# Attention products of two heads at a time with feature-major results, and a limit on how many weight units are asked for ahead of a loop

## The chip, the cores and the metric

The kernel runs on one core of a Trainium2 chip. The core has five engines with queues of their own: TensorE (PE, with its weight loads shown apart as PEld), VectorE (DVE), ScalarE (ACT), GpSimd (POOL) and SyncE (SP), and 16 DMA engines. The metric is device time in microseconds (us): the median of several runs, lower is better.

## The reference

Two blocks on 256 tokens of 1024 features, in float32. The first is a diffusion-style block: a gated feed-forward network, a mixer and another feed-forward network. Its mixer adds a gated recurrence (split here into products within and between chunks) and a windowed attention with 8 query heads on 2 key heads, whose keys are the 128-token band and 256 context tokens:

```
s_band = einsum('bkgnqd,bknsd->bkgnqs', qb, kb) * scale        # where(valid), and s_ctx on the context
p = softmax_with_sink(concatenate([s_band, s_ctx]), sink)
o = einsum(p[..., :3*BLOCK], vb) + einsum(p[..., 3*BLOCK:], vc)
```

The second block runs two layers. Each has four attention branches side by side (latent attention of 4 heads, stick-breaking attention of 4, sliding-window attention with sinks of 8 heads on 2 key heads, differential attention of 4), gates and merges them, normalizes, and sends each token to 2 of 32 experts:

```
merged = gate_a * (o_a @ w_br_a) + gate_b * (o_b @ w_br_b) + gate_c * (o_c @ w_br_c) + gate_d * (o_d @ w_br_d)
x = layer_norm(DN_ALPHA * x + merged @ w_out);  x = layer_norm(DN_ALPHA * x + grouped_moe(x))
```

## The kernel before

Tokens lie as two tiles of 128 (index `i`). Weights come from memory in units of 128 x 1024 floats (512 KB). The class `Weights` keeps a list of all units in the order of use. `_load` asks for the next unit as soon as a slot (a buffer) is free, on SP's DMA queue; `_prepare` splits a unit into a high part (ACT, L97) and a low part (DVE or POOL, L98) where products are made of three passes (`mm3`, L151 to L153); `more` gives slots back. The units of the experts are used unsplit.

A scheduler sets the order of instructions on each engine before the run. It places projections (L151 to L153), which wait for nothing but weights, between the steps of the attention.

*First block.* `attention(i)` goes head by head: scores of one head (L835; K is 64 rows, so half the rows of the array, upper for s = 0, lower for s = 1), mask, maximum, exponential (L838 to L844), four transposes (L847), a copy, four products with the values (L851: 128 stationary columns, 64 moving ones), all heads into one PSUM tile with tokens on partitions. At the end one multiplication divides by the softmax sums, and `rows_T` transposes the result to feature-major for the output projection. `within(i)`, the recurrence inside chunks (L877 to L913), is a second generator that is drawn three steps for each head. Both take PSUM tiles of the tag `ax`, of which there are four.

*Second block.* In each layer the sliding window (L1258, L1272), the differential part (L1296, L1315), the stick-breaking part (L1339, L1340, L1360) and the latent part (L1413, L1420) write token-major results into `OT[i]`; after the gates they are transposed (L1453) and split.

*Experts.* `expert_pass` handles 8 quads of 4 experts, 24 units a quad: `prepare` gathers tokens by a one-hot product (L1624, L1633), `first` (L1662) and `second` (L1689) put four experts side by side, each on 32 columns of the array. There are 41 slots for units. After the fourth quad (unit 96) `more_rounds` reads a count into a register on all engines and runs a loop for experts with more than 32 tokens; in these runs the loop's body is not entered, but SP must have its loads landed and all engines meet there (L1753, L1754). SP's part of that stands behind the loads that were asked for by then:

```
with tc.issue_after(st.loads[st.taken + 8].ins):
    nr = nc.values_load(rounds[0:1, 0:1], min_val=0, max_val=S // CAP - 1)
with tc.For_i(0, nr, 1):
```

Of the kernel before, what the change touches and what calls it, by code (L numbers as in the profile page):

```python
# [18 lines left out]
D = 1024  # L19
# [5 lines left out]
ETB = 2  # L25
QUADS = 8
RING3 = 12
# [4 lines left out]
class Weights:  # L32
# [4 lines left out]
    def __init__(self, nc):  # L37
        self.nc = nc
        self.seq = []
        self.free = {"raw": deque(), "split": deque()}  # L40
        self.loaded = self.ready = self.taken = 0
        self.raw, self.parts, self.held, self.out = {}, {}, {}, []
        self.names = 0
        self.loads = []
        self.end = {}
# [76 lines left out]
def build(tc, A, out):  # L122
# [203 lines left out]
    def gate_rows(pool, i, r, w):  # L326
# [6 lines left out]
        return G  # L333

# [492 lines left out]
    def attention(i):  # L827
        nm = pa.tile([128, 8], FT, name="nmax", bufs=2)
        den = pa.tile([128, 8], FT, name="den", bufs=2)
        PO = pmm("ax")  # L830
        for j in range(4):
            for s in range(2):
                h = j + 4 * s
                P = pmm("ax")
                PE.matmul(P, lhsT=aqT[64 * s:64 * s + 64, j, 128 * i:128 * i + 128], rhs=akT[64 * s:64 * s + 64, :],  # L835
                          start=True, stop=True)
                mk = P[:, 128:256] if i == 0 else P[:, 0:128]
# [10 lines left out]
                pT = pa.tile([128, 512], FT, name="pT", bufs=2)  # L848
# [11 lines left out]
        V.tensor_tensor(out=o.rearrange("p (h d) -> p h d", h=8), in0=PO.rearrange("p (h d) -> p h d", h=8),  # L860
                        in1=den[:, :, None].to_broadcast([128, 8, 64]), op=OP.mult)
        rows_T(oaT, i, o)
# [274 lines left out]
    for l in range(2):  # L1137
# [10 lines left out]
        OT = [pL.tile([128, 1280], FT, name=f"o{i}") for i in range(2)]  # L1148
# [93 lines left out]
        project("swk", 1)  # L1242
        if l:
            rows_on()
        for i in range(2):
# [3 lines left out]

            PO = pmm("ax")  # L1250
            den = pa.tile([128, 8], FT, name="den", bufs=3)
            for s in range(2):
                for g0 in range(0, 4, per):
                    P = pmm("ax")
                    Pv = P.rearrange("p (a b) -> p a b", a=per)
                    sc = pa.tile([128, 512], FT, name="sc", bufs=2).rearrange("p (a b) -> p a b", a=per)
                    for j in range(per):
                        PE.matmul(Pv[:, j, :], lhsT=qs["swq"][64 * s:64 * s + 64, g0 + j, qsl],  # L1258
                                  rhs=qs["swk"][64 * s:64 * s + 64, 0, :keys], start=True, stop=True)
                    for j in range(per):  # L1260
                        V.scalar_tensor_tensor(sc[:, j, :], dist[:, 1, 128 * i:128 * i + keys], -sw_slopes[4 * s + g0 + j],
                                               Pv[:, j, :], op0=OP.mult, op1=OP.add)
# [6 lines left out]
                    T = transposed([pr[:, j, 128 * b:128 * b + 128] for j in range(per) for b in blocks(i)])  # L1269
                    for j in range(per):  # L1270
                        for b in blocks(i):
                            PE.matmul(PO[:, 64 * (h0 + j):64 * (h0 + j) + 64], lhsT=T[j * (i + 1) + b],  # L1272
                                      rhs=swv[:, b, 64 * s:64 * s + 64], start=b == 0, stop=b == i)
            V.reciprocal(den, den)
            V.tensor_tensor(out=OT[i][:, 512:1024].rearrange("p (h d) -> p h d", h=8), in0=PO.rearrange("p (h d) -> p h d", h=8),
                            in1=den[:, :, None].to_broadcast([128, 8, 64]), op=OP.mult)
# [7 lines left out]
        for i in range(2):  # L1284
            keys = 128 * (i + 1)
            qsl = slice(128 * i, 128 * i + 128)

            PO = pmm("ax")
            for g0 in range(4):
                n = 2  # L1290
                o = 32 * g0
                P = pmm("ax")
                Pv = P[:, :2 * keys].rearrange("p (a b) -> p a b", a=n)
                sc = pa.tile([128, 512], FT, name="sc", bufs=2)[:, :2 * keys].rearrange("p (a b) -> p a b", a=n)
                for j in range(n):
                    PE.matmul(Pv[:, j, :], lhsT=qs["dfq"][o:o + 32, j, qsl], rhs=qs["dfk"][o:o + 32, j, :keys],  # L1296
                              start=True, stop=True, tile_position=(o, 0))
# [19 lines left out]
            od = OT[i][:, 1024:1280]  # L1317
# [16 lines left out]
        aTs = []  # L1334
        for h in range(4):
            o = 64 * (h % 2)
            q_, k_ = qs["sbq"][o:o + 64, h // 2, :], qs["sbk"][o:o + 64, h // 2, :]
            P = pmm("ax")
            PE.matmul(P[:, 0:256], lhsT=k_[:, 0:128], rhs=q_, start=True, stop=True)  # L1339
            PE.matmul(P[:, 256:384], lhsT=k_[:, 128:256], rhs=q_[:, 128:256], start=True, stop=True)  # L1340
# [15 lines left out]
        for i in range(2):  # L1356
            PO = pmm("ax")
            for h in range(4):
                for b in blocks(i):
                    PE.matmul(PO[:, 64 * h:64 * h + 64], lhsT=aTs[h][:, 128 * (i + b):128 * (i + b) + 128],  # L1360
                              rhs=vv[:, b, 64 * h:64 * h + 64], start=b == 0, stop=b == i)
            V.tensor_copy(OT[i][:, 256:512], PO[:, :256])

# [38 lines left out]
        for i in range(2):  # L1402
# [6 lines left out]
            for g0 in range(0, 4, per):  # L1409
# [8 lines left out]
                for j in range(per):  # L1418
                    for b in blocks(i):
                        PE.matmul(PO[:, 64 * (g0 + j):64 * (g0 + j) + 64], lhsT=T[j * (i + 1) + b],  # L1420
                                  rhs=mv[:, b, 64 * (g0 + j):64 * (g0 + j) + 64], start=b == 0, stop=b == i)
            V.reciprocal(den[:, :4], den[:, :4])
            V.tensor_tensor(out=OT[i][:, 0:256].rearrange("p (h d) -> p h d", h=4), in0=PO[:, :256].rearrange("p (h d) -> p h d", h=4),
                            in1=den[:, 0:4, None].to_broadcast([128, 4, 64]), op=OP.mult)
# [23 lines left out]
        for k in range(0, 10, 2):  # L1448
            P = pmm("ax")
            for kk in range(2):  # L1450
                for i in range(2):
# [164 lines left out]
        def expert_pass(place, w13_of, w2_of, after, main):  # L1616
# [92 lines left out]
            for p in range(QUADS):  # L1709
# [40 lines left out]
        def more_rounds():  # L1750

            with tc.issue_after(st.loads[st.taken + 8].ins):
# [13 lines left out]

        expert_pass(place, taken, taken, st.more, True)
# [85 lines left out]
def layout(I):  # L1853
# [26 lines left out]
    for n, z in (("w_oa", I["w_o_attn"][0]), ("w_oh", I["w_o_hgrn"][0])):  # L1880
# [63 lines left out]
    for l in range(2):  # L1944
# [17 lines left out]
        b = np.concatenate([J["w_br_" + n][l] for n in "abcd"], 0)  # L1962
# [26 lines left out]
```

## Time and profile before

| | |
|---|---|
| median of 3 runs | 2072.26 us (2071.64 to 2073.36) |
| the profiled execution, its own time | 2079.71 us |
| its span, first to last instruction | 2077.9 us |
| mean granted TensorE clock | 0.947 of 2.4 GHz |
| busy: PE, DVE, ACT, POOL | 88%, 53%, 38%, 11% |
| read from memory | 433.51 MB, 209 GB/s over the span |

The profile lists instructions with line numbers of the kernel (L835 is line 835). An f32 matmul is two instructions there, so "x8" of them is four products. A matmul's duration includes its way through the array; consecutive ones overlap, so the cost of one is read from start to start. PEclk is the granted share of full clock, 1.00 for 2.4 GHz and 0.50 for 1.2 GHz.

### The profile page before, as it was taken

Reading aid. Unit: us, or ns where it says so; the run is one execution under the profiler, and the core shown is the slowest. Engines: PE = TensorE matmul, PEld = TensorE weight load, DVE = VectorE, ACT = ScalarE, POOL = GpSimd, SP = SyncE. Lnnn points to the kernel's source line nnn. Section 1 sums busy time; section 2 is a strip of 40 time slices with the busy share of each in tenths; the row PEclk is TensorE's granted clock in tenths of the full one; section 3 lists DMA queues with packets and bytes.
Section 4 is the critical chain, followed back from the end, with each engine's and each line's share of the span. In section 5 each row is a group of like instructions: output and inputs, shape, how many; then the busy total and the mean of one; then the engine's idle time right before and its main releaser. Section 6 shows DMA issues by size and latency. Waiting matters only on the chain. (4 is left out here: it accounts for less than half of the span.)

```text
span 2077.9 us, 29422 instructions
## 1 busy us (share of the span) xinstructions
PE 1823.1 (88%) x11398; PEld 1437.9 (69%) x11398; DVE 1098.2 (53%) x2088; ACT 788.1 (38%) x1363; POOL 238.1 (11%) x170
## 2 busy tenths in 40 slices
PE   6989999989999987999999997963979999988096
PEld 2767788877878786998888996522438899853052
DVE  4775465584656567554668556210257864631023
ACT  3443222453443435444445644210234574321011
POOL 2553000131132221000100011000010000200000
PEclk9999999999999999999999999986999999989598
DMA  8543565442232234555434378897964435889987
GB/s 310 193 149 119 187 234 205 147 157 82 71 125 82 72 103 143 185 190 189 146 113 135 122 265 321 345 413 302 414 241 142 132 123 203 305 333 413 377 338 280
DMA packets 120118, 436.61 MB, mean 210 GB/s; under 512 B 13616, under 2 KB 13664, under 8 KB 119968
## 3 DMA queue, kind: packets, MB, share of 16 engines
q1 hardware_dynamic: 116208, 422.63, 55.3%
q0 software_dynamic: 2608, 8.32, 1.2%
q10 hardware_dynamic: 1152, 3.67, 0.5%
q8 instruction: 94, 1.54, 0.3%
q14 instruction: 56, 0.46, 0.1%
HBM read 433.51 MB, written 1.05 MB: 209 GB/s over the span
## 5 line engine op out<-in xcount | busy, mean ns | idle before, releaser
L98 DVE TENSOR_TENSOR split7l<-raw,split7h 128x1024 fp32r<-128x1024 f32 x98 | 124.6, 1271 | 113.1 <-ACT split7h L97 112.9
L98 DVE TENSOR_TENSOR split6l<-raw,split6h 128x1024 fp32r<-128x1024 f32 x99 | 128.4, 1297 | 85.4 <-ACT split6h L97 82.4
L97 ACT ACTIVATE split6h<-raw 128x1024 fp32r<-128x1024 f32 x102 | 107.9, 1057 | 162.5 <-issue 58.9
L97 ACT ACTIVATE split7h<-raw 128x1024 fp32r<-128x1024 f32 x101 | 106.8, 1057 | 165.0 <-PE mm L153 65.4
L1633 PE MATMUL ax<-OH,X 128*128 128x128 f32 x512 | 71.7, 307 | 100.0 <-DVE OH L1624 97.9
L1633 PEld LDWEIGHTS ax<-OH,X 128*128 128x128 f32 x512 | 70.1, 222 | 105.1 <-DVE OH L1624 98.7
L1662 PE MATMUL ax<-raw,xg 128*32 128x512 f32 x1024 | 133.9, 595 | 4.1 <-DMA raw<-in_moe 4.1
L1662 PEld LDWEIGHTS ax<-raw,xg 128*32 128x32 f32 x1024 | 33.9, 109 | 91.3 <-issue 61.4
L586 DVE SCALAR_TENSOR_TENSOR xn<-raw,xn 128x1024 f32<-128x1024 f32 x56 | 84.9, 1517 | 22.0 <-DMA raw<-in_w_mod 21.3
L363 ACT ACTIVATE xg<-ax,cols 128x128 f32<-128x128 f32 x64 | 24.0, 456 | 176.6 <-PE ax L1633 176.6
L1689 PE MATMUL ax<-raw,ehT 128*32 128x512 f32 x512 | 70.7, 608 | 18.6 <-ACT ehT L144 17.7
L583 POOL TENSOR_TENSOR raw<-raw,xn 128x1024 f32<-128x1024 f32 x24 | 72.5, 3033 | 73.8 <-DVE xn L586 70.1
L1696 DVE SCALAR_TENSOR_TENSOR yl<-ax,gsl,yh 128x512 fp32r<-128x512 f32 x32 | 24.0, 751 | 87.4 <-ACT yh L1695 83.7
L1671 DVE TENSOR_TENSOR ehs<-ax,ehs 128x256 f32<-128x256 f32 x16 | 6.8, 424 | 117.5 <-ACT ehs L1670 117.5
L1624 DVE TENSOR_TENSOR OH<-iota,place 128x128 f32<-128x128 f32 x32 | 7.8, 286 | 110.8 <-SPq L1754 98.7
L1689 PEld LDWEIGHTS ax<-raw,ehT 128*32 128x32 f32 x512 | 16.7, 110 | 57.8 <-issue 28.0
L153 PE MATMUL mm<-hThi,split7l 128*128 128x512 f32 x128 | 52.5, 410 | 3.9 <-DVE split7l L98 3.9
L153 PE MATMUL mm<-hxhi,split7l 128*128 128x256 f32 x192 | 54.8, 286 | 1.3 <-POOL split7l L98 1.2
L151 PE MATMUL mm<-hxhi,split6h 128*128 128x256 f32 x192 | 54.5, 284 | 1.7 <-ACT split6h L97 1.7
L151 PE MATMUL mm<-hThi,split6h 128*128 128x512 f32 x128 | 51.7, 404 | 4.3 <-ACT hThi L144 2.2
L1670 ACT ACTIVATE ehs<-ax 128x256 f32<-128x256 f32 x16 | 6.1, 384 | 129.5 <-PE ax L1662 129.5
L152 PE MATMUL mm<-hxlo,split7h 128*128 128x256 f32 x192 | 54.7, 285 | 0.7 <-POOL hxlo L380 0.7
(876 smaller groups left out, 5776.3 us busy)
## 6 DMA issues: line engine op xcount, KB each, us to landing
raw<-in_moe SPq DMA_DIRECT2D x384, 512.0 KB, 10.1
raw<-in_f_in SPq DMA_DIRECT2D x88, 512.0 KB, 4.2
raw<-in_w_gate SPq DMA_DIRECT2D x64, 512.0 KB, 3.4
raw<-in_w_mod SPq DMA_DIRECT2D x56, 512.0 KB, 4.3
raw<-in_f_out SPq DMA_DIRECT2D x55, 512.0 KB, 4.2
raw<-in_w_out SPq DMA_DIRECT2D x24, 512.0 KB, 6.0
raw<-in_w_br SPq DMA_DIRECT2D x20, 512.0 KB, 3.5
raw<-in_w_ada SPq DMA_DIRECT2D x16, 512.0 KB, 10.0
```

The source lines that it names most:

```text
L97: nc.scalar.activation(hi, x, AF.Copy)
L98: (nc.gpsimd if self.seq[i][1] == "pool" else nc.vector).tensor_tensor(out=lo, in0=x, in1=hi, op=OP.subtract)
L151: PE.matmul(o, lhsT=lh, rhs=rh, start=first, stop=False)
L152: PE.matmul(o, lhsT=lh, rhs=rl, start=False, stop=False)
L153: PE.matmul(o, lhsT=ll, rhs=rh, start=False, stop=last)
L363: SC.activation(o, p, AF.Identity, bias=b, scale=g)
L583: GP.tensor_tensor(out=w, in0=w, in1=crow[r], op=OP.mult)
L586: V.scalar_tensor_tensor(mscr, w, 1.0, crow[r], op0=OP.mult, op1=OP.mult, accum_out=m)
L1633: PE.matmul(P[:, 128 * b:128 * b + 128], lhsT=X[:, i, 128 * d:128 * d + 128], rhs=OH[:, i, :], start=i == 0, stop=i == 1)
L1662: PE.matmul(P[32 * s:32 * s + 32, :], lhsT=xg[:, k, 32 * s:32 * s + 32], rhs=ws[s](kk), start=k == 0, stop=k == DT - 1, tile_position=(0, ...
L1689: PE.matmul(P[32 * s:32 * s + 32, :], lhsT=d_["hT"][:, k, 32 * s:32 * s + 32], rhs=ws[s](k), start=k == 0, stop=k == 1, tile_position=(0, ...
L1696: V.scalar_tensor_tensor(yl, P, d_["gsl"], yh, op0=OP.mult, op1=OP.subtract)
```

## The change

Five edits:

- The scores of two heads are issued one after the other before the softmax of either, in the first block (s = 0 and s = 1), the sliding window, the differential part (32-row tiles) and the stick-breaking part.
- The products with the values swap sides: the values (64 columns) are stationary, the transposed probabilities (128 columns) move, and the two heads of a pair write the upper and lower 64 partitions of one PSUM tile, features on partitions. In the latent part too.
- Division by the softmax sums moves behind that: `over_rows` spreads 1/sum over the partitions with small products (64 columns each), a copy on ACT and a multiplication on DVE. The transposes of these results go: `rows_T` in the first block, four of five groups at L1453. The results have tiles of their own (`swo`, `smo`); the output weights are laid out to match on the host.
- The generators of the first block are drawn 5 times with 6 steps of `within`, instead of 9 times with 3.
- `_load` stops at `limit`, which is set to 16 units beyond the fourth quad before the pass and lifted after the loop; SP's part of the loop stands behind the last of these.

```diff
+AHEAD = 16
     def _load(self):
-        while self.loaded < len(self.seq):
+        while self.loaded < min(len(self.seq), self.limit):
...
+    def over_rows(o, p, c, n):
+        R = pmm("ax")
+        for j in range(n):
+            for s in range(2):
+                PE.matmul(R[64 * s:64 * s + 64, 128 * j:128 * j + 128], lhsT=c[:, s, j:j + 1].to_broadcast([128, 64]), rhs=ident,
+                          start=True, stop=True, tile_position=(0, 64 * s))
+        copy_act(o, R[:, :128 * n].rearrange("p (a b) -> p a b", a=n))
+        V.tensor_tensor(out=o, in0=p.rearrange("p (a b) -> p a b", a=n), in1=o, op=OP.mult)
...
         for j in range(4):
-            for s in range(2):
-                h = j + 4 * s
-                P = pmm("ax")
+            Ps = [pmm("ax") for _ in range(2)]
+            for s, P in enumerate(Ps):
                 PE.matmul(P, lhsT=aqT[64 * s:64 * s + 64, j, 128 * i:128 * i + 128], rhs=akT[64 * s:64 * s + 64, :],
                           start=True, stop=True)
+            pTs = []
+            for s, P in enumerate(Ps):
+                h = j + 4 * s
...
-                for b in range(4):
-                    PE.matmul(PO[:, h * 64:h * 64 + 64], lhsT=pT[:, b * 128:b * 128 + 128], rhs=av[:, b, s * 64:s * 64 + 64],
-                              start=b == 0, stop=b == 3)
-                yield
+                pTs.append(pT)
+            for b in range(4):
+                for s in range(2):
+                    PE.matmul(PO[64 * s:64 * s + 64, 128 * j:128 * j + 128], lhsT=av[:, b, s * 64:s * 64 + 64],
+                              rhs=pTs[s][:, b * 128:b * 128 + 128], start=b == 0, stop=b == 3, tile_position=(0, 64 * s))
+            yield
...
-        rows_T(oaT, i, o)
+        over_rows(o, PO, den.rearrange("p (s j) -> p s j", s=2), 4)
...
-        for n in range(9):
+        for n in range(5):
             next(a)
-            for _ in range(3):
+            for _ in range(6):
                 next(w, None)
...
-        for k in range(0, 10, 2):
-            P = pmm("ax")
-            for kk in range(2):
-                for i in range(2):
-                    c = (k + kk) * 128
-                    PE.transpose(P[:, kk * 256 + i * 128:kk * 256 + i * 128 + 128], OT[i][:, c:c + 128], ident)
-            split(oT[k // 2][:, 0], oT[k // 2][:, 1], P.rearrange("p (a b) -> p a b", a=2))
+        P = pmm("ax")
+        for kk in range(2):
+            for i in range(2):
+                PE.transpose(P[:, kk * 256 + i * 128:kk * 256 + i * 128 + 128], OT[i][:, 128 * kk:128 * kk + 128], ident)
+        for t, o in zip(oT, (smo[:, 0:2], smo[:, 2:4], swo[:, 0:2], swo[:, 2:4], P.rearrange("p (a b) -> p a b", a=2))):
+            split(t[:, 0], t[:, 1], o)
...
                     more_rounds()
+                    st.limit = 1 << 30
+                    st.more()
                     prepare(p + 1)
...
-            with tc.issue_after(st.loads[st.taken + 8].ins):
+            with tc.issue_after(st.loads[st.limit - 1].ins):
...
+        st.limit = st.taken + 12 * QUADS + AHEAD
         expert_pass(place, taken, taken, st.more, True)
```

The sliding-window, differential, stick-breaking and latent parts change in the same way as `attention`.

Three places show what the scheduler makes of it. The first is SP's queue at the loop of the first layer. The numbers after `raw` are those of the slot and of the tile. Before, the last loads ahead of the loop are:

```order
L80 DMA raw34_12131<-in_moe 128x1024
L80 DMA raw0_12141<-in_moe 128x1024
...
L80 DMA raw26_12193<-in_moe 128x1024
L80 DMA raw37_12195<-in_moe 128x1024
L80 DMA raw38_12197<-in_moe 128x1024
L1753 TENSOR_LOAD rounds_11540
L1754 COMPARE_AND_BRANCH
```

After the change:

```order
L83 DMA raw32_12076<-in_moe 128x1024
L83 DMA raw46_12091<-in_moe 128x1024
L83 DMA raw47_12093<-in_moe 128x1024
L83 DMA raw48_12095<-in_moe 128x1024
L1790 TENSOR_LOAD rounds_11562
L1791 COMPARE_AND_BRANCH
```

25 loads that stood ahead of the loop stand behind it (the first of them into slot 49); 16 beyond unit 96 stay ahead. The second layer's loop is the same.

The second place is PE's order in a pair of heads of the first block's second half. `pr` are the probabilities, `pT` their transposes, `Mh`, `lfh` and `lfl` belong to `within`. Before, one head after its transposes, and the scores of the next:

```order
L847 MATMUL ax<-ident,pr 128x128 x4
L877 MATMUL ax<-Mh,lfh_3679 128x512
L878 MATMUL ax<-Mh,lfl_3680 128x512
L877 MATMUL ax<-Mh,lfh_3679 128x512
L878 MATMUL ax<-Mh,lfl_3680 128x512
L851 MATMUL ax<-av,pT 128x64 x4
L877 MATMUL ax<-Mh,lfh_3679 128x512
L878 MATMUL ax<-Mh,lfl_3680 128x512
L835 MATMUL ax<-akT,aqT 128x512
```

After, both heads' transposes (L865) and their eight products with the values (L871):

```order
L865 MATMUL ax<-ident,pr 128x128 x4
L155 MATMUL mm<-hxlo,split6h 128x256
L156 MATMUL mm<-hxhi,split6l 128x256
L865 MATMUL ax<-ident,pr 128x128 x4
L898 MATMUL ax<-Mh,lfh_3924 128x512
L871 MATMUL ax<-pT,av 64x128
L899 MATMUL ax<-Mh,lfl_3925 128x512
L898 MATMUL ax<-Mh,lfh_3924 128x512
L871 MATMUL ax<-pT,av 64x128 x7
L899 MATMUL ax<-Mh,lfl_3925 128x512
```

Two projections stand between the two heads' transposes; the value products of both heads form one group, cut once by a product of `within`.

The third place is PE's order at the end of the first block's attention (second half). Before, from the last but one head's values on:

```order
L851 MATMUL ax<-av,pT 128x64 x4
L901 MATMUL ax<-W,U 128x128 x4
L835 MATMUL ax<-akT,aqT 128x512
L847 MATMUL ax<-ident,pr 128x128 x4
L901 MATMUL ax<-W,U 128x128 x4
L851 MATMUL ax<-av,pT 128x64 x4
L901 MATMUL ax<-W,U 128x128 x4
L901 MATMUL ax<-qT,ksum 128x128 x4
L823 MATMUL ax<-ident,oatt 128x128 x4
L911 MATMUL ax<-hv_3506,AT 128x128
```

After, the products of `over_rows` (L344), the end of `within`, and projections behind it:

```order
L922 MATMUL ax<-qT,ksum 128x128 x4
L344 MATMUL ax<-ident,den 64x128 x8
L154 MATMUL mm<-hxhi,split7h 128x256
...
L932 MATMUL ax<-hv_3506,AT 128x128
L934 MATMUL ax<-S_3749,VS_4997 128x128
L934 MATMUL ax<-S_3974,VS_4999 128x128
L155 MATMUL mm<-hxlo,split7h 128x256
L156 MATMUL mm<-hxhi,split7l 128x256
L154 MATMUL mm<-hxhi,split7h 128x256
L155 MATMUL mm<-hxlo,split7h 128x256
```

Before, no projection is left there; after, 184 stand behind the attention's last product.

## Rows read from the trace of the kernel before

**Rows 1.** The page's first part: busy time, share, instructions.
```profile
PE 1823.1 (88%) x11398; PEld 1437.9 (69%) x11398; DVE 1098.2 (53%) x2088; ACT 788.1 (38%) x1363; POOL 238.1 (11%) x170
```

**Rows 2.** Windows: start:end, length, busy (count) per engine, clock, DMA share, GB/s.
```profile
591.00:741.00 150.00, 141.50 (x888) 116.24 (x888) 87.90 (x152) 62.43 (x117) 42.13 (x41) 0.95 0.25 86
1034.00:1220.00 186.00, 182.85 (x1360) 167.28 (x1359) 120.36 (x247) 101.70 (x202) 1.19 (x2) 1.00 0.40 134
1100.00:1120.00 20.00, 18.60 (x138) 17.05 (x139) 18.36 (x45) 8.95 (x17) 0.00 (x0) 1.00 0.43 135
```

**Rows 3.** Waits: waiting engine, line, releaser: total us, times, longest.
```profile
DVE OH L1624 <- SPq L1754: 98.7, 2, 49.4
```

**Rows 4.** SP's queue at the first loop, by line: duration (ns), first and last start.
```profile
L80 SPq DMA_DIRECT2D raw<-in_moe x25: 327/328/328, 1395.1 to 1425.3; - x25
L1754 SPq EVENT_SEMAPHORE  x20: 17/28/28, 1434.1 to 1439.0; - x20
L1753 SPq SEQ_ASSERT x1: 28/28/28, 1439.5 to 1439.5; - x1
L80 SPq DMA_DIRECT2D raw<-in_moe x3: 336/413/431, 1445.9 to 1446.7; - x3
```

**Rows 5.** The same at the second loop.
```profile
L1753 SPq SEQ_ASSERT x1: 24/24/24, 1975.8 to 1975.8; - x1
L80 SPq DMA_DIRECT2D raw<-in_moe x5: 342/430/518, 1982.0 to 1983.8; - x5
```

**Rows 6.** Windows of the expert stage around the first loop.
```profile
1400.00:1420.00 20.00, 0.00 (x0) 0.00 (x0) 0.00 (x0) 0.00 (x0) 0.00 (x0) 0.50 1.03 415
1420.00:1440.00 20.00, 3.28 (x15) 3.28 (x16) 0.90 (x4) 0.00 (x0) 0.00 (x0) 0.50 0.69 279
1440.00:1460.00 20.00, 18.64 (x161) 11.25 (x159) 5.67 (x22) 4.89 (x13) 0.00 (x0) 0.93 0.67 256
1460.00:1480.00 20.00, 18.70 (x156) 9.45 (x148) 4.38 (x12) 3.81 (x9) 0.50 (x1) 1.00 1.03 413
```

**Rows 7.** Timeline of PE, scores and the row behind: start, length, instruction.
```profile
613.72 1.12 PE L835 MATMUL ax<-akT,aqT 64*128 64x512 f32 x2
614.77 0.39 PE L153 MATMUL mm<-hxhi,split7l 128*128 128x256 f32 x1
...
1057.43 1.13 PE L1258 MATMUL ax<-swk,swq 64*128 64x256 f32 x4
1058.49 0.38 PE L152 MATMUL mm<-xlo,split22h 128*128 128x256 f32 x1
...
1061.77 0.70 PE L1258 MATMUL ax<-swk,swq 64*128 64x256 f32 x2
1062.40 0.44 PE L1208 MATMUL ax<-ident,pr 128*128 128x128 f32 x2
```

**Rows 8.** Timeline of PE: value products, the row behind, transposes of results.
```profile
603.87 1.00 PE L851 MATMUL ax<-av,pT 128*128 128x64 f32 x8
604.68 0.48 PE L877 MATMUL ax<-Mh,lfh 128*128 128x512 f32 x1
...
1221.73 1.91 PE L1453 MATMUL ax<-ident,o 128*128 128x128 f32 x16
```

**Rows 9.** Timeline of PE's weight loads in the experts, tiles of 32 columns.
```profile
1444.37 0.13 PEld L1662 LDWEIGHTS ax<-raw,xg 128*32 128x32 f32 x4 [0.30 <-issue]
1444.80 0.13 PEld L1662 LDWEIGHTS ax<-raw,xg 128*32 128x32 f32 x4 [0.30 <-issue]
```

**Rows 10.** Timeline of one head's softmax in the first block.
```profile
607.41 0.30 DVE L838 TENSOR_TENSOR ax<-ax,amask 128x128 f32<-128x128 f32 x1 [1.22 <-PE ax L835]
...
608.96 0.69 ACT L844 ACTIVATE pr<-ax,nmax 128x512 f32<-128x512 f32 x1 [1.96 <-issue]
...
609.98 0.60 PE L847 MATMUL ax<-ident,pr 128*128 128x128 f32 x4
```

**Rows 11.** The end of the first block's attention: window, and a row of PE.
```profile
720.00:740.00 20.00, 15.13 (x75) 12.99 (x74) 11.93 (x25) 4.66 (x10) 3.42 (x4) 0.74 0.07 26
...
731.50 0.66 PE L847 MATMUL ax<-ident,pr 128*128 128x128 f32 x4 [2.93 <-ACT pr L844]
```

More of the change, by code (lines that the diff above doesn't have):

```diff
@@ L25 @@
 ETB = 2
+PTB = 2
 QUADS = 8
+AHEAD = 16
 RING3 = 12
@@ L44, in __init__ @@
         self.loads = []
+        self.limit = 1 << 30
         self.end = {}
@@ L1147, in build @@
         xt2 = [(xT, 0), (xT, 1)]
-        OT = [pL.tile([128, 1280], FT, name=f"o{i}") for i in range(2)]
+        OT = [pL.tile([128, 256], FT, name=f"o{i}") for i in range(2)]
         at = ExitStack()
@@ L1242, in build @@
         project("swk", 1)
+        swo = pL.tile([128, 4, 256], FT, name="swo")
         if l:
@@ L1268, in build @@
                     V.tensor_tensor(out=den[:, h0:h0 + per], in0=den[:, h0:h0 + per], in1=es_[:, :per], op=OP.add)
[L1269 to L1273, printed above, removed]
+                    Ts.append(transposed([pr[:, j, 128 * b:128 * b + 128] for j in range(per) for b in blocks(i)]))
+                for j in range(per):
+                    for b in blocks(i):
+                        for s in range(2):
+                            PE.matmul(PO[64 * s:64 * s + 64, 128 * (g0 + j):128 * (g0 + j) + 128], lhsT=swv[:, b, 64 * s:64 * s + 64],
+                                      rhs=Ts[s][j * (i + 1) + b], start=b == 0, stop=b == i, tile_position=(0, 64 * s))
             V.reciprocal(den, den)
-            V.tensor_tensor(out=OT[i][:, 512:1024].rearrange("p (h d) -> p h d", h=8), in0=PO.rearrange("p (h d) -> p h d", h=8),
-                            in1=den[:, :, None].to_broadcast([128, 8, 64]), op=OP.mult)
+            over_rows(swo[:, :, qsl], PO, den.rearrange("p (s j) -> p s j", s=2), 4)
         vv = unit([2, 512], "vv")
@@ L1316, in build @@
                                   start=b == 0, stop=b == i)
-            od = OT[i][:, 1024:1280]
+            od = OT[i]
             copy_act(od, PO[:, :256])
@@ L1334, in build @@
         aTs = []
+        Pz = {}
         for h in range(4):
[L1336 to L1340, printed above, removed]
+            if h % 2 == 0:
+                for hh in (h, h + 1):
+                    Pz[hh] = pmm("ax")
+                for kc, qc, n in ((0, 0, 256), (128, 128, 128)):
+                    for hh in (h, h + 1):
+                        o = 64 * (hh % 2)
+                        q_, k_ = qs["sbq"][o:o + 64, hh // 2, :], qs["sbk"][o:o + 64, hh // 2, :]
+                        c = 2 * kc
+                        PE.matmul(Pz[hh][:, c:c + n], lhsT=k_[:, kc:kc + 128], rhs=q_[:, qc:qc + n], start=True, stop=True)
+            P = Pz.pop(h)
             z = pa.tile([128, 384], FT, name="sbz", bufs=4)
@@ L1355, in build @@
             aTs.append(z)
-        for i in range(2):
-            PO = pmm("ax")
-            for h in range(4):
+        PO = pmm("ax")
+        for p in range(2):
+            for i in range(2):
                 for b in blocks(i):
-                    PE.matmul(PO[:, 64 * h:64 * h + 64], lhsT=aTs[h][:, 128 * (i + b):128 * (i + b) + 128],
-                              rhs=vv[:, b, 64 * h:64 * h + 64], start=b == 0, stop=b == i)
-            V.tensor_copy(OT[i][:, 256:512], PO[:, :256])
+                    for s in range(2):
+                        h = 2 * p + s
+                        PE.matmul(PO[64 * s:64 * s + 64, 256 * p + 128 * i:256 * p + 128 * i + 128],
+                                  lhsT=vv[:, b, 64 * h:64 * h + 64], rhs=aTs[h][:, 128 * (i + b):128 * (i + b) + 128],
+                                  start=b == 0, stop=b == i, tile_position=(0, 64 * s))
+        smo = pL.tile([128, 4, 256], FT, name="smo")
+        V.tensor_copy(smo[:, 2:4, :], PO.rearrange("p (a b) -> p a b", a=2))
         mq, mk = unit([4, 256], "mq"), unit([4, 256], "mk")
@@ L1417, in build @@
                 T = transposed([pr[:, j, 128 * b:128 * b + 128] for j in range(per) for b in blocks(i)])
[L1418 removed]
+                for j in range(0, per, 2):
                     for b in blocks(i):
[L1420 to L1421 removed]
+                        for s in range(2):
+                            h = g0 + j + s
+                            PE.matmul(PO[64 * s:64 * s + 64, 64 * (g0 + j):64 * (g0 + j) + 128], lhsT=mv[:, b, 64 * h:64 * h + 64],
+                                      rhs=T[(j + s) * (i + 1) + b], start=b == 0, stop=b == i, tile_position=(0, 64 * s))
             V.reciprocal(den[:, :4], den[:, :4])
[L1423 to L1424 removed]
+            over_rows(smo[:, 0:2, qsl], PO[:, :256], den[:, 0:4].rearrange("p (j s) -> p s j", s=2), 2)
         gts = []
```

51 lines of the change are left out of this document (30 added, 21 removed).

## The prediction

> **What bounds the kernel now.** I read the page first: TensorE (PE) is busy for 88% of the span [rows 1]. Then the table of windows, because that share is a mean over unlike stages. In the first block's attention PE is busy 141.5 of 150 us, and in the first layer's attention of the second block 182.85 of 186 [rows 2]: there PE's own work sets the time, and the reader is to see that VectorE (DVE), at 120 of 186, is not far behind; in 1100 to 1120 it is at 18.36 of 20. In the expert stage it is the other way round: PE stands still for a whole window and the DMA engines are at their limit (share 1.03) before and after [rows 6]. The list of waits then names one wait that repeats: DVE, and PE behind it, sit 98.7 us in two waits for SP at the overflow loop [rows 3].
>
> What that loop costs is not 98.7 us. SP issues 25 more units after the sixteenth, one every 1.26 us (1395.1 to 1425.3), waits until all have landed (first of the loop's semaphores at 1434.1), meets the other engines, is free at 1439.5, and its next load starts only at 1445.9 [rows 4]. The DMA engines work through most of PE's wait. They are idle from about 1433.4 to 1447: 0.69 and 0.67 of two windows of 20 us against 1.03 when full, so some 13.5 us [rows 6]. Since loading bounds the stage, that idle stretch is what the end feels.
>
> **The change, part by part.**
>
> *The limit at the loop.* In the order before, 41 units stand between unit 96 and the loop, which is every slot there is. When SP is free at 1439.5 no slot is: the next load must wait until PE has gathered the fifth quad's rows and used four units. In the order after, 16 stand there, so 25 slots are free when SP leaves the loop. The landing, the meeting and SP's way out (1434.1 to 1439.5) remain; the wait for a slot, 1439.5 to 1445.9, goes: 6.4 us. In the second layer it is 1975.8 to 1982.0: 6.2 [rows 5]. Together **-12.6**. PE's wait becomes shorter by 25 units, but PE then waits for the same units later on, so this adds nothing. What is behind SP is only loads. Bounds: 0, if something else delays the restart, and -38.6, if the whole hole between two loads went (20.6 less 1.26, twice); I take the middle value, since in the order after the load right behind the loop goes to a slot that is free by then.
>
> *The products in pairs, as PE time.* Two prices serve for all. A pair of 64x256 f32 products takes 1.06 us and one alone 0.63 [rows 7]: 0.43 a product, and 0.20 for entering and leaving the narrow tile. A 64x512 one takes 1.05, which is 0.85 and the same 0.20 [rows 7]. I take 0.22, half of 0.43, for 128 columns; the four products of 64 columns at 603.87 take 0.81, so 0.20 to 0.22 each [rows 8].
> Before: scores 16 x 0.85, then in both layers 32 x 0.22 and 32 x 0.43 (sliding window and differential together), 8 x 0.43 and 8 x 0.22 (stick-breaking): 39.6, and 60 entries by the order, 12.0; values 160 x 0.22 = 35.2; 40 transposes that go, at 1.91/16 = 0.12 [rows 8]: 4.8. Sum 91.6.
> After: the scores' 39.6, the values' 160 products, now of 128 columns with half the stationary columns, 35.2, and 64 new products of `over_rows`, 14.1: 88.9. If two tiles of the array work side by side that is 44.5, and the order has 80 entries, 16.0: 60.5. So **-31.1**. If they do not: 104.9, or +13.3.
> Which of the two? The trace shows four column tiles of the experts side by side: four weight loads every 0.43 us, the time of one pass of 512 columns [rows 9]. So I take the column pairs as certain almost. Two row tiles side by side no row of before shows: there the bounds are 0 and the half. I take the half, since their scores go to two PSUM tiles and the columns' case is the nearest row.
> The Trainium skill speaks against part of this. Its page "TensorE: Matmul & The Clock Gate" (Part 3, The mechanism) says matmuls start and end strictly in program order. An f32 product is two instructions here, and if both passes of one head stand ahead of the other head's, only the second pass of one and the first of the other overlap, and a lone pair takes three passes for two. The experts' rows show passes that alternate between tiles; so I leave that to the rivals.
>
> *What comes back as waits.* The order puts just enough projections between a pair of scores and its transposes to cover the softmax of heads done one after another. A head's mask, maximum and scaling take 1.55 us on DVE (607.41 to 608.96) and is transposed at 609.98 [rows 10]. With both scores ready together, the second head's transposes can start some 1.5 us after the first's: about 4.1 us after the scores. In most pairs of the first block the order has some 20 projections of 256 columns (0.12 us each) and four transposes ahead of them, 2.9 us. That returns about 1.1 us in five of eight pairs, none in the two with long covers, little in the last: 5.5. In the differential part DVE is at 18.36 of 20 already [rows 2] and the order after squeezes the same DVE work into 231 projections where 369 stood: I take the whole gain of its scores, 14.0 - 8.4 = 5.6, as returned. Of the other streams of the two layers (18.6) I take a quarter, 4.1. **+15.2**; bounds 0 and the whole 44.5.
>
> *The tail of the first attention.* Before, the last pairs of the second half have no projection left between scores and transposes. PE is busy 15.13 of 20 us in 720 to 740, its mean clock is 0.74, and one wait alone is 2.93 [rows 11]. A mean of 0.74 between full and half speed is 10.4 us at the lower level, 1.2 GHz; 4.9 of them idle, the other 5.5 cost 2.75. After, 184 projections are still to come when this attention ends. **-7**, a little below 4.9 + 2.75; bounds 0 and -7.6.
>
> *Costed at nothing.* One more copy on ScalarE (ACT) for each `over_rows`: ACT is busy 101.7 of 186 us [rows 2], PE's projections hide it; on the path it would be 0.6 us ten times. The hand-made PSUM use: a pair holds two score tiles and the output, three of four; this is a rival below.
>
> **Sum.** -31.1 + 15.2 - 7 - 12.6 = -35.5. The profiled execution's own time is 2079.7 (span 2077.9), so 2044.2; it lies 7.4 above the median 2072.3, so the median should be about **2037 us**.
>
> **Rivals.**
> - *Nothing comes back:* the softmax stays ahead of PE everywhere. -50.7, 2022. For it: PE hardly waits in the layers now (3.15 of 186). Against: DVE at 18.36 of 20.
> - *Row tiles do not overlap:* the scores' half, 19.8, is lost, and only 4 come back. -31.1 + 19.8 + 4 - 7 - 12.6 = -26.9, 2045. For it: no row shows them.
> - *Both passes of one head stand ahead of the other's:* a group then takes half a product more: 8 x 0.43 in the first block, 8 x 0.11 and 8 x 0.21 in the differential part, some 0.11 in the other 56, together 12; 4 of them out of the waits. -31.1 + 12 + 11.2 - 7 - 12.6 = -27.5, 2045. Against: the alternating passes of [rows 9]. This is what the skill's rule above would do here.
> - *No pair overlaps:* the change would not do what it says. +13.3 - 7 - 12.6 = -6.3, 2066. Against: [rows 9].
> - *The hole at the loop only moves:* SP's first loads find the queue no earlier, and that part is worth 0: 2049. Against: 25 free slots.
> - *Slower:* the pair's three PSUM tiles leave one of the four `ax` for transposes and for `within`, so PE stands in order behind a tile not yet released. There are 26 pairs (8, and 9 in each layer). It takes 2.1 us in each of them to eat 50.7 and 4 more; at 2.5 us, 65 us, the time is 2087. Against: a tile is free again once the first head's exponential has read it, which is before its transposes.
>
> **How the numbers follow.** Forecast 0.50 (its own range 2026 to 2048), nothing back 0.14, row tiles 0.11, passes in order 0.05, no pair 0.07, loop 0.08, slower 0.05. 0.2% is 4.1 us, about what a measurement of this kernel can tell from no change. Faster takes all but the last and a part of "no pair": 0.93; within 0.2% 0.03; slower 0.04. The range reaches from below "nothing back" to short of "no pair", 2018 to 2060, and leaves out about 0.17.
>
> **What would show it.** The wait of DVE for SP at the loop near 18 us each (49.4 less 25 units of 1.26), and SP's first load within 1 us of its way out. Two scores' instructions of one pair starting within some 20 ns of each other; the two heads' value products too. The window of the first attention near 137 us for the same work, without a half-speed stretch at its end. New short waits of PE for exponentials in front of the second head's transposes. If the starts of a pair lie a whole pass apart, the first price is wrong; if those waits are long, the +15.2 is.

## The result, and the profile after

| | before | changed | ratio, 95% interval |
|---|---|---|---|
| median | 2072.81 us (2071.64 to 2076.09, 4 runs) | 2042.72 us (2040.91 to 2048.34, 4 runs) | 0.9854, 0.9841 to 0.9867 |
| the same kernel once more (e8), with runs of before beside it | 2072.09 us (9 runs) | 2045.48 us (4 runs) | 0.9870, 0.9855 to 0.9885 |
| the profiled execution, its own time | 2079.71 us | 2043.18 us | |

Faster by 1.3 to 1.5%, 27 to 30 us; the range of the forecast, 2018 to 2060, holds both. Lines 151 to 153 of the kernel before are 154 to 156 now, L835 is L850, L847 is L865, L851 is L871, L901 is L922, L1208 is L1229, L1296 is L1319, L1753 and L1754 are L1790 and L1791. L922 are products of the recurrence, L914 POOL's multiplications for them, L865 and L1229 transposes of probabilities, L1380 products of the stick-breaking part.

The page's first part, against [rows 1]: TensorE (PE) has about as much busy time in a shorter span.

```profile
PE 1832.6 (90%) x11486; PEld 1415.3 (69%) x11486; DVE 1085.5 (53%) x2086; ACT 785.5 (38%) x1369; POOL 238.6 (12%) x170
```

The table of windows of the changed kernel: start:end, length, busy (count) of PE, PEld, DVE, ACT and POOL, granted clock, DMA share, GB/s.

```profile
589.00:742.00 153.00, 142.20 (x1015) 117.50 (x1014) 93.91 (x182) 70.07 (x129) 42.91 (x45) 0.99 0.29 98
700.00:720.00 20.00, 19.35 (x168) 17.68 (x167) 14.45 (x36) 8.46 (x16) 5.82 (x8) 1.00 0.25 83
1020.00:1204.00 184.00, 177.61 (x1400) 162.41 (x1399) 119.54 (x251) 100.84 (x206) 1.96 (x2) 0.97 0.40 133
1050.00:1100.00 50.00, 46.13 (x327) 41.56 (x324) 38.32 (x104) 23.45 (x56) 0.00 (x0) 0.90 0.32 106
1084.00:1086.00 2.00, 0.20 (x2) 0.06 (x1) 1.94 (x3) 0.00 (x0) 0.00 (x0) 1.00 0.10 41
1088.00:1098.00 10.00, 9.31 (x40) 8.25 (x41) 8.10 (x18) 2.81 (x7) 0.00 (x0) 0.50 0.18 54
1098.20:1108.20 10.00, 9.85 (x80) 8.96 (x79) 7.07 (x14) 4.71 (x11) 0.00 (x0) 1.00 0.44 134
1360.00:1380.00 20.00, 7.23 (x30) 2.12 (x25) 1.50 (x2) 1.38 (x2) 0.00 (x0) 0.78 1.03 405
1380.00:1400.00 20.00, 13.28 (x102) 8.62 (x102) 3.37 (x14) 1.78 (x5) 0.00 (x0) 0.71 0.62 237
1400.00:1420.00 20.00, 18.64 (x137) 10.03 (x130) 4.40 (x13) 3.81 (x9) 0.00 (x0) 1.00 1.03 417
```

The reader is to see three things. The first attention's end (700 to 720) runs at full clock with PE busy 19.35 of 20; before it was 15.13 at 0.74 [rows 11]. Around the loop only one window of 20 us falls short of the full DMA share, where two did [rows 6]. And a stretch is new in the layers: PE idle in 1084 to 1086, then ten microseconds at a clock of 0.50 with half as many instructions in as much time (40 against 80 right behind it); the layers of before had a clock of 1.00 throughout ([rows 2] for the first).

PE's timeline (start, length, instruction): scores of a pair, the value products of a pair, and the row behind each.

```profile
589.08 1.13 PE L850 MATMUL ax<-akT,aqT 64*128 64x512 f32 x4
590.13 0.51 PE L155 MATMUL mm<-split7l,hxhi 128*128 128x512 f32 x1
...
633.68 0.43 PE L871 MATMUL ax<-pT,av 128*64 128x128 f32 x2
634.04 0.50 PE L898 MATMUL ax<-Mh,lfh 128*128 128x512 f32 x1
634.48 1.09 PE L871 MATMUL ax<-pT,av 128*64 128x128 f32 x14
635.49 0.50 PE L899 MATMUL ax<-Mh,lfl 128*128 128x512 f32 x1
...
1032.63 1.14 PE L1277 MATMUL ax<-swk,swq 64*128 64x256 f32 x8
1033.69 0.50 PE L156 MATMUL mm<-split22h,xlo 128*128 128x512 f32 x1
```

Two heads' scores (x4) take 1.05 us from their start to the next row's; one head's (x2) took 1.05 before [rows 7]. The first passes of the two start at 589.075 and 589.082 in the trace, 7 ns apart, the second passes at 589.609 and 589.615. So two row tiles do run side by side, and the passes alternate. Two column tiles do as well: fourteen instructions of the values take 1.01 us to the next row's start (634.48 to 635.49), and their starts come in twos, 7 ns apart (634.475 and 634.482).

SP's queue at the two loops, by line: duration (ns), first and last start. L1791 is the meeting of the engines, L1790 SP's way out, L83 the loads behind it.

```profile
L1791 SPq EVENT_SEMAPHORE  x20: 17/28/28, 1385.3 to 1389.1; - x20
L1790 SPq SEQ_ASSERT  x1: 32/32/32, 1389.6 to 1389.6; - x1
L83 SPq DMA_DIRECT2D raw<-in_moe x4: 342/430/432, 1389.7 to 1391.0; - x4
...
L1790 SPq SEQ_ASSERT  x1: 28/28/28, 1914.4 to 1914.4; - x1
L83 SPq DMA_DIRECT2D raw<-in_moe x5: 342/432/597, 1914.4 to 1916.2; - x5
```

The first load follows SP's way out at once (1389.6 and 1389.7; 6.4 us lay between before [rows 4], 6.2 at the second loop [rows 5]). But for a few small transfers, the DMA engines stand still for 5.8 us at each loop (1384.8 to 1390.6 in the trace at the first) where it was 11.9 (1434.9 to 1446.8).

The list of waits of the changed kernel: the loop, then PE in the first attention (581 to 742), then PE in the first layer.

```profile
DVE OH L1659 <- SPq L1791: 36.8, 2, 18.5
...
PE ax L922 <- POOL W L914: 3.9, 4, 2.5
PE ax L865 <- ACT pr L862: 3.0, 4, 1.5
...
PE ax L1229 <- DVE pr L1333: 2.9, 2, 2.6
PE ax L1380 <- DVE sbe L1378: 2.0, 2, 1.0
```

The wait at the loop is 18.5 us, as the prediction had it. The waits in attention are few. The longest are one for POOL in the recurrence (L922), which the prediction does not have, and one for DVE in the differential part (L1229), where it had taken the gain of the scores as lost.

**Stretches.** All these kernels issue 7,356 projection instructions, in the same order but for at most 119 places, so the one of the same number marks the same place in each; of the two marks of an expert stage one is another instruction. Lengths in us between such marks, in single profiles:

| stretch | before | changed | again (e8) | e1 | e2 | e3 | e4 | e5 |
|---|---|---|---|---|---|---|---|---|
| ahead of the first attention | 583.3 | 581.5 | 577.1 | 583.4 | 579.2 | 576.6 | 579.5 | 582.5 |
| first attention and its projections | 236.9 | 225.9 | 224.9 | 236.8 | 222.0 | 226.6 | 217.9 | 219.4 |
| attention of layer 1 | 209.5 | 205.4 | 206.3 | 209.4 | 206.0 | 202.4 | 206.0 | 202.4 |
| expert stage 1 | 259.0 | 252.0 | 252.8 | 251.9 | 256.2 | 254.9 | 252.3 | 254.7 |
| attention of layer 2 | 208.9 | 205.1 | 205.2 | 208.9 | 204.5 | 201.9 | 204.5 | 201.9 |
| expert stage 2 | 241.5 | 233.1 | 233.5 | 234.4 | 239.2 | 234.0 | 235.9 | 233.4 |

The first line holds no edit and varies by 7 us between executions, so one profile can't weigh a few microseconds there. The layers repeat to 1.5 us where the code is the same; the first attention, the same in the changed kernel, e8, e2 and e3, lies between 222.0 and 226.6.

### The profile page after: what moved, and what is told of

It is laid out like the page before. It is cut to its first block, busy times and chain, and to the rows that moved or that the text cites. A ratio compares the mean times of both kernels' runs of the same rounds, so it can differ in the third digit from the quotient of the medians.

```text
span 2041.4 us, 29593 instructions
## 1 busy us (share of the span) xinstructions
PE 1832.6 (90%) x11486; PEld 1415.3 (69%) x11486; DVE 1085.5 (53%) x2086; ACT 785.5 (38%) x1369; POOL 238.6 (12%) x170
## 3 DMA queue, kind: packets, MB, share of 16 engines
HBM read 433.51 MB, written 1.05 MB: 213 GB/s over the span
## 5 line engine op out<-in xcount | busy, mean ns | idle before, releaser
L1697 PE MATMUL ax<-raw,xg 128*32 128x512 f32 x1024 | 166.1, 596 | 7.0 <-DMA raw<-in_moe 7.0
L1697 PEld LDWEIGHTS ax<-raw,xg 128*32 128x32 f32 x1024 | 37.2, 109 | 107.2 <-issue 59.6
L1724 PE MATMUL ax<-raw,ehT 128*32 128x512 f32 x512 | 77.1, 607 | 16.6 <-ACT ehT L147 15.6
L156 PE MATMUL mm<-hThi,split6l 128*128 128x512 f32 x128 | 53.0, 414 | 4.8 <-DVE split6l L101 4.8
L154 PE MATMUL mm<-hxhi,split7h 128*128 128x256 f32 x192 | 55.2, 288 | 0.0
```

The costliest lines, as they stand in the source:

```text
L154: PE.matmul(o, lhsT=lh, rhs=rh, start=first, stop=False)
L156: PE.matmul(o, lhsT=ll, rhs=rh, start=False, stop=last)
L1697: PE.matmul(P[32 * s:32 * s + 32, :], lhsT=xg[:, k, 32 * s:32 * s + 32], rhs=ws[s](kk), start=k == 0, stop=k == DT - 1, tile_position=(0, ...
L1724: PE.matmul(P[32 * s:32 * s + 32, :], lhsT=d_["hT"][:, k, 32 * s:32 * s + 32], rhs=ws[s](k), start=k == 0, stop=k == 1, tile_position=(0, ...
```

## The experiments

**e1, the limit alone**, in the kernel before:

```diff
+AHEAD = 16
-        while self.loaded < len(self.seq):
+        while self.loaded < min(len(self.seq), self.limit):
...
                     more_rounds()
+                    st.limit = 1 << 30
+                    st.more()
...
-            with tc.issue_after(st.loads[st.taken + 8].ins):
+            with tc.issue_after(st.loads[st.limit - 1].ins):
...
+        st.limit = st.taken + 12 * QUADS + AHEAD
```

> The kernel before, with the limit at the loop alone. Theory A (the parts are independent; the limit gives back the wait for a free slot): the expert stages of the changed kernel gained 5.5 and 7.2 us against the kernel before, so 2072.8 - 12.7 = 2060, and SP's first load within 1 us of its way out of the loop. Theory B (the loop profits only because attention leaves the queue in another state; the hole only moves): no change, 2072 to 2073.

2064.32 us, ratio 0.9953 (0.9939 to 0.9967): -9.7 us, between 6.8 and 12.6. SP's queue in this kernel, first and second loop:

```profile
L1757 SPq SEQ_ASSERT  x1: 32/32/32, 1406.2 to 1406.2; - x1
L82 SPq DMA_DIRECT2D raw<-in_moe x6: 335/432/506, 1406.3 to 1408.7; - x6
...
L1757 SPq SEQ_ASSERT  x1: 28/28/28, 1935.2 to 1935.2; - x1
L82 SPq DMA_DIRECT2D raw<-in_moe x4: 342/432/1701, 1935.3 to 1937.9; - x4
```

Theory A in its mechanism: the load comes 0.1 us after the way out, and attention is untouched (236.8, 209.4, 208.9). The size is some 3 us below its 12.7, which lies just outside the interval.

**e2, the pairs alone**: the changed kernel with the lines on `limit` taken out, SP's part of the loop behind the load of nine units past the fourth quad, as before.

> The changed kernel without the limit. Theory A (the parts add up): 2042.7 + 12.7 = 2055.4, with waits of 49 us at the loop and a load 6 us after SP's way out. Theory B (the parts overlap, and one hides what the other costs): 2048 or less, or 2060 and more.

2048.73 us, ratio 0.9886 (0.9862 to 0.9909): -23.6 us, between 18.9 and 28.6. The expected 2055.4 is just outside. Against e1 and the whole: 9.7 + 23.6 = 33.3, and the whole is 27 to 30; the intervals of the two parts (2.9 and 4.9 to either side) leave room for that, so a part that hides another is not shown, nor ruled out: from e2 to the changed kernel the ratios give the limit only 3 to 7 us, while the stages give 10 and e2's first attention, the same code, is 3 to 4 us shorter in its profile. SP's queue shows one thing in which A's figure was off:

```profile
L1788 SPq SEQ_ASSERT  x1: 32/32/32, 1415.6 to 1415.6; - x1
L83 SPq DMA_DIRECT2D raw<-in_moe x7: 328/424/436, 1420.9 to 1423.9; - x7
...
L1788 SPq SEQ_ASSERT  x1: 28/28/28, 1945.1 to 1945.1; - x1
L83 SPq DMA_DIRECT2D raw<-in_moe x6: 342/432/623, 1950.3 to 1952.7; - x6
```

The wait for a slot is 5.3 and 5.2 here, not 6.4 and 6.2, and the expert stages, whose code is that of before, took 256.2 and 239.2, together 5 us less than in the profile of before. Over the profiles the stages without the limit (two profiles) average 257.6 and 240.4, with it (eight) 252.9 and 234.1: 11.0 us for the limit, near e1's 9.7.

**e3, differential scores head by head**, all else paired:

```diff
-                if g0 % 2 == 0:
-                    for g in (g0, g0 + 1):
-                        Ps[g] = pmm("ax")[:, :2 * keys].rearrange("p (a b) -> p a b", a=n)
...
-                Pv = Ps.pop(g0)
+                o = 32 * g0
+                Pv = pmm("ax")[:, :2 * keys].rearrange("p (a b) -> p a b", a=n)
+                for j in range(n):
+                    PE.matmul(Pv[:, j, :], lhsT=qs["dfq"][o:o + 32, j, qsl], rhs=qs["dfk"][o:o + 32, j, :keys],
+                              start=True, stop=True, tile_position=(o, 0))
```

> The changed kernel, but the scores of the differential part go head by head as before; all else stays paired. Theory A (the pair there brings one wait of 2.6 us in each layer, and the half clock behind it costs more than the pair saves): the half-speed stretches of 10.2 and 13.7 us go, which gives 5.1 and up to 6.8; the wait for the softmax falls from 2.9 to about 0.6 in each layer, -4.6; the scores cost 7.0 again, where a pair at full clock takes about 3.9, +6.2. 2042.7 - 11.9 - 4.6 + 6.2 = 2032. Theory B (only PE's own work counts, the wait would come anyway): the scores go from 5.2 back to 7.0 in each layer, 2046.

2036.39 us, ratio 0.9824 (0.9797 to 0.9851). Taking the pairs of this part away made it faster: 6 us against the first measurement of the changed kernel, whose interval (from 0.9841) it just touches, 9 against the second, from which it is clear, and 3.0 to 3.9 and 3.2 us in the two layers by the table. Its windows and PE's waits in the first layer:

```profile
1050.00:1100.00 50.00, 47.99 (x365) 44.32 (x364) 39.49 (x92) 24.18 (x51) 0.00 (x0) 1.00 0.45 146
...
PE ax L1229 <- DVE pr L1329: 0.7, 4, 0.2
```

The wait is gone, the clock is 1.00 where it was 0.90, and 365 instructions stand in the 50 us where 327 did. That is theory A, with its 10.7 some 4 us too large by the stages; B's 2046 is out. Counted from start to start, the projections and the other products of the first layer lost 2.8 us of slowness and PE 2.0 of idle time, for 1.8 that the scores cost more. I had taken half of the whole slow stretch as its price; PE also waits and stands in it.

The wait itself, in the changed kernel. PE's timeline, then DVE's:

```profile
1083.54 0.66 PE L1340 MATMUL ax<-vv,pT 128*128 128x64 f32 x4
1086.81 0.44 PE L1229 MATMUL ax<-ident,pr 128*128 128x128 f32 x2 [2.61 <-DVE pr L1333]
...
1090.39 0.41 PE L155 MATMUL mm<-split22l,cThi 128*128 128x256 f32 x1
1090.61 0.41 PE L156 MATMUL mm<-split22h,cTlo 128*128 128x256 f32 x1
```

```profile
1083.92 1.22 DVE L1405 TENSOR_TENSOR mk<-rt 32x1024 f32<-32x1024 f32 x1
1085.17 0.35 DVE L1332 TENSOR_SCALAR pr<-pr,dend 128x256 f32<-128x256 f32 x1
1085.55 0.69 DVE L1418 TENSOR_TENSOR rt<-mm,cs 32x512 f32<-32x512 f32 x1
1086.27 0.48 DVE L1333 SCALAR_TENSOR_TENSOR pr<-pr,dend 128x256 f32<-128x256 f32 x1
```

DVE does not rest for a moment; the second head's probabilities stand behind rotary work of the latent part (L1405, L1418), and only six projections are left in PE's queue to cover that. Behind it, at a clock of 0.50, a projection takes 0.21 us from start to start (1090.393 to 1090.606 in the trace), at full clock 0.12.

**e4, the recurrence drawn by three again**:

```diff
                 pTs.append(pT)
+                if s == 0:
+                    yield
...
-        for n in range(5):
+        for n in range(9):
             next(a)
-            for _ in range(6):
+            for _ in range(3):
```

> The changed kernel, but in the first block the recurrence is drawn three steps at a time again, after the first head of a pair and after the second. Theory A (PE's idle time in the first block's attention comes from steps drawn by six, which wait for POOL one behind the other): the 5.2 us in front of those products fall below 1, the half-speed stretch behind the longest goes (3.4 us at half, so 1.7), 2042.7 - 6 = 2037. Theory B (the wait is that of the second head's transposes for its exponential, as the prediction had it): the steps put between the two heads cover part of it, the first block's waits for POOL stay, 2041 to 2043.

2038.45 us, ratio 0.9830 (0.9806 to 0.9853): by the ratios 5 us below the first measurement of the changed kernel, 8 below the second, and the first attention is 7 to 8 us shorter than in the two profiles of the changed kernel, 4 to 9 shorter than in the four with the same code there. PE's waits in it:

```profile
PE ax L865 <- ACT pr L862: 1.3, 4, 0.5
PE ax L924 <- POOL W L916: 0.8, 3, 0.4
```

3.9 for POOL became 0.8, and the exponentials 1.3 instead of 3.0; no stretch below full clock is left there. Theory A. Drawn by six, several steps that each need two POOL multiplications (0.91 and 0.98 us before the longest wait) come one behind the other; by three they have a head's products between them. Before the longest wait POOL also has 1.39 us of another multiplication (L953, from 619.49), so the steps by six need not be all of it.

**e5, both of these**.

> The changed kernel with both: differential scores head by head, and the recurrence drawn three steps at a time. Theory A (two separate stalls with a half-speed stretch behind each): the gains add; the stages of the two single edits were 3.0 and 3.3 us (differential, the two layers) and 8.3 us (first block) shorter than those of the changed kernel, of which the timed medians bore out 6.2 and 5: about 2042.7 - 11 = 2031.5. Theory B (PE's saved time meets another limit, so that only one of them counts): 2036 or more.

2032.38 us, ratio 0.9804 (0.9789 to 0.9819): theory A, the two gains add as far as the times can tell (B's 2036 is just outside), and the stages show both, the first attention at 219.4 and the layers at e3's 202.4 and 201.9. This is the fastest of the kernels here, 40 us below the kernel before and 10 to 13 below the changed one, clear of both measurements of that.

**e6, value products head after head**:

```diff
-            for b in range(4):
-                for s in range(2):
+            for s in range(2):
+                for b in range(4):
```

and the same in the sliding window.

> The changed kernel, but in the first block and the sliding window all value products of one head stand ahead of those of the other in PE's queue (128 of the 160 pairs' products; the two column tiles are as before). Theory A (a product may start early in its own column tile wherever it stands in the queue): no change, 2042.7. Theory B (the queue is followed in order, and only neighbours in different tiles run side by side): 112 products lose their partner, at 0.11 us each in the trace of the changed kernel, +12: 2055, and starts of 0.22 us from one to the next within a head.

2044.60 us, ratio 0.9870 (0.9853 to 0.9887), like the changed kernel. Theory B's 2055 is out, but theory A is not what the rows show either:

```profile
599.84 1.61 PE L871 MATMUL ax<-pT,av 128*64 128x128 f32 x16
...
610.10 1.09 PE L871 MATMUL ax<-pT,av 128*64 128x128 f32 x8
613.16 1.09 PE L871 MATMUL ax<-pT,av 128*64 128x128 f32 x8
630.88 1.58 PE L871 MATMUL ax<-pT,av 128*64 128x128 f32 x16
```

One head's eight instructions take 1.09 us, as many as fourteen that alternate; both heads' sixteen take 1.58 or 1.61, where twice the eight would be some 2.0 (eight more of 0.11) and full overlap 1.1. The overlap is half lost; why not all of it or none, no run shows. The end hardly feels it: the alternating order is split by the scheduler into two groups (x2 and x14, 0.43 and 1.09), each with its entry, and counted from start to start the values cost 4.7 us more in all three stretches. That this is less than the spread of the runs is all that the time says.

**e7, 32 units ahead of the loop** (`AHEAD = 32`).

> The changed kernel with 32 units ahead of the loop in place of 16: 9 slots are free behind the loop in place of 25. Theory A (what counts is that a slot is free when SP leaves the loop, for the 5 to 6 us until PE gives back the next ones): 9 loads of 1.26 us cover 11 us, so no change, 2042.7, while DVE waits some 38 us at the loop. Theory B (the gain goes with the number of free slots): two thirds of it are lost, 2048 to 2051.

2040.97 us (2037.84 to 2050.86, 5 runs), ratio 0.9851 (0.9832 to 0.9871): theory A. The profile is of the longest run. The wait at the loop and SP's queue behind it:

```profile
DVE OH L1659 <- SPq L1791: 77.5, 2, 39.2
...
L1790 SPq SEQ_ASSERT  x1: 28/28/28, 1415.5 to 1415.5; - x1
L83 SPq DMA_DIRECT2D raw<-in_moe x15: 327/427/637, 1415.6 to 1428.5; - x15
```

Engines wait twice as long as with 16 and the time is the same, and the DMA engines stand still as long as with 16 (5.6 and 5.4 us in the trace): the wait was never the price, the empty queue was.

**e8, the changed kernel once more**.

> The changed kernel itself once more, to be compared with the others of this call on one chip. All theories: 2042.7, between 2040 and 2046.

2045.48 us (2042.98 to 2046.08), ratio 0.9870, as expected: the second line of the first table.

## Why the prediction was right, and where its terms were off

- **What bounds it.** Right. PE's work in attention and loading in the expert stages could be changed apart (e1, e2), and what PE waited at the loop did not matter (e7).
- **PE's products, 91.6 to 60.5, -31.1.** The overlap is as assumed, rows included. Counted over the three attention stretches from each instruction's start to the next one's, less idle time: scores 51.5 to 32.2, values 37.2 to 25.8, `over_rows` 8.6, transposes -5.4. That is 94.1 to 66.6, -27.5. Some 3 us of the difference are scores at half clock: those of the differential part take 5.2 and 5.7 us in the two layers, the sliding window's, of the same sizes and number, 3.8.
- **+15.2 for what comes back, -7 for the tail.** Their sum, +8.2, came out (+8.5: idle time +4.5, slower work +4.0), but by another way, so that it fits is luck. (+15.2 also holds a slip: a quarter of 18.6 is 4.65, not 4.1.) The first attention with its projections became 11.0 us shorter, where 13 had been expected (150 to 137). The tail did become full, but the first attention's idle time stayed at 22.2 us: the recurrence, drawn by six, stood behind POOL instead, an edit that the prediction left unpriced. The exponentials took 3.0 us of the 5.5 forecast. In the layers the waits grew by 2.5 and 2.0 us only; the rest is the half clock behind one of them. The prediction had said that DVE is full in the differential part and the gain there would be lost. It was more than lost: e3 is faster without that pair. The step that failed is the one that priced a returned wait at its own length: in the first layer 2.0 us of idle time brought 2.8 of slower work with them (e3).
- **How the tail was read.** The prediction put PE's 4.9 idle us into the 10.4 at half clock. The windows of before show them apart:

```profile
728.00:730.00 2.00, 0.57 (x2) 0.00 (x0) 2.00 (x5) 0.00 (x0) 1.26 (x2) 1.00 0.00 0
...
734.00:736.00 2.00, 2.00 (x11) 2.00 (x11) 1.11 (x2) 0.00 (x0) 0.00 (x0) 0.50 0.00 0
```

PE stood still at full clock and was busy at half clock (722.6 to 726.0 and 732.8 to 739.6 in the trace, 10.2 us). The tail so held 4.9 and, as an estimate, half of 10.2: about 10, where the prediction has 7.65 and takes 7. Part of the difference stands in the products' count above, which takes each instruction as long as it ran.

- **-12.6 for the loop.** The mechanism and the two waits are as predicted; the size is 9.7 (e1; its interval reaches 12.6). The two profiles without the limit differ in the wait for a slot (6.4 and 6.2 in the one I read, 5.3 and 5.2 in e2's); whether that is the execution or the other kernel ahead of the loop is not shown. The DMA engines' idle time at a loop, 13.5 by the prediction's two windows, is 11.9 in the trace.
- **From one execution to the median.** The sum of -35.5 fits the two profiled executions (2079.7 to 2043.2, -36.5). The median moved by 27 to 30. I took the 7.4 us by which the profiled execution was long off the end, as if they would stay; part of them lay in the terms themselves, in the expert stages above all: e1's profile, like that of before up to there, is 14.2 us shorter in them, where the timed runs give 9.7. So 4 to 5 of the 5.7 us from 2037 to 2042.7 may be this.
- **Rivals.** Row tiles overlap (589.075 and 589.082). The passes alternate, so "both passes of one head ahead" is out. Pairs overlap, the hole at the loop did not just move (e1), and PE stood idle before no score of the changed kernel, so none waited for a PSUM tile. "Nothing comes back" is refuted by e3 and e4, and e5's 2032 shows how near to it one can get.

On the order in the queue: e6 shows that a product starts in its own column tile while earlier ones of the other tile are still to start. In its first group the second head's first pass starts at 600.356; the first head's sixth to eighth, which stand ahead of it in the queue, start at 600.432, 600.541 and 600.650. (The second head's is the one that has a wait for a semaphore of its own; behind it the starts form two series, each 0.109 us from one to the next.) The page "TensorE: Matmul & The Clock Gate" of the Trainium skill (Part 3, The mechanism) has matmuls start and end strictly in program order; by that rule e6 would have been theory B, 2055. The measurement decides: within a tile the starts kept the order here, between tiles they did not.

## What to carry to other kernels

Pair small products only where another engine can keep up with both results; where that engine is full, as DVE is here in the differential part, the pair makes it late for the second, and PE pays the wait and a slow stretch with it. Look at a meeting point of engines not by how long they wait, but by what the busiest resource does meanwhile, here whether the loads can start again at once. Size a term from more than one execution, or from the shorter one, before it is set against a median.

## What the runs showed of the hardware

- With the same wait of 2.61 us of PE in the differential part came a stretch at 1.2 GHz of 10.2 or 13.7 us in all twelve layers in which it stood (six profiles with the pair), begun during the wait or up to 1.2 us behind it, and none in the four layers of e3 and e5 without it. With the wait of 2.4 to 2.5 us in the recurrence came 3.4 us at that level in the changed kernel and e6, 6.8 in e3, and none in e2, e7 and e8. So the price of a short stall is not its length, and it differs from place to place and run to run.
- Nor does a slow stretch need a stall. Behind the attention of a layer e8 has PE busy without a gap and yet 6.8 us at 1.2 GHz:

```profile
1203.00:1213.50 10.50, 10.50 (x95) 10.50 (x93) 7.34 (x10) 4.46 (x6) 2.25 (x2) 1.00 0.98 367
1213.50:1220.30 6.80, 6.80 (x34) 6.80 (x34) 2.80 (x5) 1.36 (x2) 1.22 (x1) 0.50 1.02 410
```

The changed kernel, the same program, has none there. From the attention of layer 1 to its experts it takes 68.9 us, e4 and e5 with 3.4 us at that level 70.3, e7 and e8 with 6.8 us 71.6. What brings this on is open; it is part of why one kernel's profiles differ.

- At a loop whose body isn't entered the DMA engines still stood idle for 5.8 us each time in the changed kernel, from the last landing over the meeting of the engines to the first new load. The limit left that: 5.4 to 6.0 us in the profiles of e1, e7 and e8 too.
